# Rows of 1/rms for two RMS norms: by TensorE, or by a store and a repeated load through DRAM

## The chip, the cores and the metric

The kernel runs on one core of a Trainium2 chip. Its engines are TensorE (PE in the profile; its weight loads are PEld), VectorE (DVE), ScalarE (ACT), GpSimd (POOL, hardly used here) and SyncE (SP), which issues nearly all DMAs. The core has 16 DMA engines. The metric is device time in microseconds (us) of one execution, of which the median of several runs is taken. A profiled execution gives the trace; it has a time of its own, and a span, from its first to its last instruction.

## The reference

One layer of a streaming encoder, with 1024 positions and 1024 channels, in float32. What matters here:

```python
def rms_norm(x, w):
    x32 = x.astype(jnp.float32)
    y = x32 * lax.rsqrt(jnp.mean(x32 * x32, axis=-1, keepdims=True) + RMS_EPS)
    return (y * w.astype(jnp.float32)).astype(x.dtype)
...
h = rms_norm(x, norm1_w[l])
proj = h @ w_in[l]          # q, k, v, gates and branches: 8192 columns
...                         # retention heads, RG-LRU branch, merge
x = x + mix @ w_out[l]
h = rms_norm(x, norm2_w[l])
up = h @ ffn_w_up[l]
gate, val = jnp.split(up, [D_FF], axis=-1)
gate = causal_depthwise_conv(gate, ffn_conv_w[l], ffn_conv_b[l])
x = x + (jax.nn.gelu(gate) * val) @ ffn_w_down[l]
...
return rms_norm(x, norm_f_w)
```

There are three norms. The change touches how the first two get their factor 1/rms, one number for each of the 1024 positions, to where it is used.

## The kernel before, in words

**Layout.** Activations lie transposed: channels on the 128 partitions, positions along the free dimension, in two halves of 512. Each float32 operand of a large product is split into a rounded high part (on ACT, line 766) and a low part, the difference (on DVE, line 767), and every product is three passes: high by high, high by low, low by high. The large products go as jobs (`mm_fast`), each of 256 output channels by 1024 positions; a job makes 7 block products instead of 8 (a Strassen-like scheme) with sums of blocks of the weights (lines 811 to 818) and of the activations (`tsets`, `h2_steps`). A product is 12 matmuls (line 893) of 128 by 128 weights on 512 columns. A job uses three PSUM banks of six, and its results are taken out of PSUM by ACT and DVE (lines 900, 905, 914 and the job's own `emit`).

**Stages in order.** First x is loaded, both transposed (`xt`, for the operands) and plain (`x`, for the sums of squares, line 1121). The v columns of the input projection run first (`values_first`, line 1483), with the operand not yet scaled by 1/rms, since in v the positions are the output's partitions and the factor is applied behind the product. Four groups of 96 matmuls are made there, on two halves of positions and two halves of columns; in each, the weights come in eight slices of k. Meanwhile the factor is worked out and the transposed x is multiplied by the weight and by the row of 1/rms (`rescale`, line 1090), and its blocks, sums and splits are the operand h1 of the other input columns. Then come 24 jobs of the input projection, with the retention heads and the recurrent blocks spread between them, eight jobs of the two branch projections, and four of the output projection. In the last, x1 (the new residual stream) is turned back by PE transposes, stored, and its squares are summed by position (lines 1669 to 1675). The second norm is applied late: the 24 jobs of the up projection run on x1 with only the weight applied, and each result is multiplied by the row of 1/rms afterwards (`with_row`, line 1399, one multiplication for each 128 channels by 1024 positions). The convolution (lines 1737 to 1739), GeLU and the product with the other half follow, and 12 jobs of the down projection with the third norm end the kernel.

**How 1/rms becomes a row.** The factor r is made with positions on partitions: a [128, 8] tile, where r[p, t] belongs to position 128 t + p (`rstd_of`, lines 989 to 995). The row that is needed has all 1024 positions along the free dimension, the same on all 128 partitions (`rowt`). `rows_of` (line 1070) gets it with PE: for each of the eight t, DVE multiplies the identity by the column r[:, t] (line 1078), and PE multiplies a matrix of ones with this diagonal matrix, as a plain float32 matmul of 128 columns (line 1079); four of them fill one PSUM bank, and ACT copies each of the two banks into a half of `rowt` (line 1080). It is called once for the first norm (line 1125) and once for the second (line 1719).

**What sets the order.** No order is written by hand. Every operation is recorded with a cost and its dependencies, and a planner (`Prog`) simulates the engines, chooses the order of each engine's queue, gives out SBUF slots (105 of 512 columns) and PSUM banks, and emits that order; each engine then runs its queue strictly in order on the chip. An operation has a latest start, worked back from who needs it and from its slack; among operations that are ready, the one with the earliest latest start goes first. Main matmuls keep their recorded order, and "side" matmuls (such as those of `rows_of`) are put between them. A DMA is planned as landing no earlier than 2.3 us after issue (line 549), its data following the DMAs before it. `run` plans up to 12 times: after each pass `blame` moves operations ahead on which PE was seen to wait, the pass with the shortest planned span is kept, and after 6 passes without a better one it stops.

Of the kernel before, what the change touches and what calls it, by code (L numbers as in the profile page):

```python
# [17 lines left out]
ALU = mybir.AluOpType  # L18

P = 128  # L20
D = 1024
T = 1024
KT = 8
# [235 lines left out]
class Prog:  # L259
# [158 lines left out]
                    push(q)  # L418

    def run(self, caps):  # L420
        best, since = None, 0
        self.prune()
        for _ in range(self.ROUNDS):
            try:
                self.forward(caps)
            except RuntimeError as e:
                if best is None:
                    raise
                print(str(e)[:60])
                break  # L430
            since += 1
            if best is None or self.span < best[0]:
                best, since = (self.span, self.order, [(v, v.slot) for o in self.order for v in o.allocs], [
                    (o, o.start, o.allocs) for o in self.order]), 0
            if since >= self.PATIENCE:
                break
            self.blame()
        self.span, self.order, slots, starts = best
        for v, i in slots:
            v.slot = i  # L440
        for o, t, a in starts:
            o.start, o.allocs = t, a
        return self.order
# [195 lines left out]
    EAGER = 12000  # L639
    EARLY = 20000  # L640
    FETCH = 24000
    ROUNDS, PATIENCE, STALL, URGE = 12, 6, 150.0, 6000.0
    BEGIN = 400
    TILE = 800.0
    LAND = 1900.0
# [8 lines left out]
    def emit(self, engines, make, behind):  # L654
        at, sent = {}, []
        for o in self.order:
# [17 lines left out]
SMALL = (("par", (P, NPAR)), ("cst", (P, NCONST)), ("st", (P, 16)), ("nst", (P, 7, 8)), ("lt", (P, 2, 8)),  # L674
         ("state0", (P, 256)), ("state1", (P, 256)), ("bst", (P, 4, 6)),
         ("mv", (P, 4, 2)), ("rs", (P, 3, 4)), ("rowt", (P, T)))
SPILL = (("og", (KT, P, T)), ("u", (KT, P, T)), ("y", (KT, P, T)), ("sg", (2, KT, P, T)), ("t1", (KT, P, T)),
         ("x1", (T, D)), ("td", (3, 4, 2, P, 2, TH)), ("to", (2, 4, 2, P, 2, TH)), ("ff", (3, 8, P, 2, 4, P)), ("rot", (4, P, T)),
         ("ss", (12, 2, P, T)), ("v", (2, KT, P, TH)))

# [20 lines left out]
TSLACK = 8000.0  # L701
# [24 lines left out]
def record(prog, fx):  # L726
    V, S, G, PE, SY = (Engine(prog, n) for n in ("DVE", "ACT", "POOL", "PE", "SP"))
    par, cst, st, nst, lt = (fx[n] for n in ("par", "cst", "st", "nst", "lt"))
    rst, bst, mv, rs = fx["rst"], fx["bst"], fx["mv"], fx["rs"]
    og_d, u_d, y_d, sg_d, t1_d, x1_d, td_d, to_d, ff_d, rot_d, ss_d, v_d = (  # L730
        fx[n + "_d"] for n in ("og", "u", "y", "sg", "t1", "x1", "td", "to", "ff", "rot", "ss", "v"))
    x, positions, normf, w_in, w_v, w_ro, w_lo, w_out, w_up, w_dn, w_gate, out, xt = (
        fx[n] for n in ("x", "positions", "normf", "w_in", "w_v", "w_ro", "w_lo", "w_out", "w_up", "w_dn", "w_gate", "out", "xt"))
    ident = cst[:, C_ID:C_ID + P]
# [4 lines left out]
    def sm():  # L739
        return Ref(VT("sm", (P, P), F32, "sc"))  # L740

    def bank(kind="g"):
        return Ref(VT(kind, (P, TH), F32, kind))

    def pc(name, i):
        return par[:, PCOL[name] + i:PCOL[name] + i + 1]

    def cut(t, h):
        if h is None:
            return t  # L750
        return t[:, h] if len(t.shape) == 3 else t[:, TH * h:TH * h + TH]
# [4 lines left out]
    @contextmanager  # L756
    def within(slack, side=False):
        was = prog.slack, prog.side
        prog.slack, prog.side = slack, side
        yield  # L760
        prog.slack, prog.side = was
# [305 lines left out]

    row = {0: fx["rowt"]}

    def rows_of(r, side, slack=1000.0):  # L1070
        one = sm()
        V.memset(one, 1.0)
        for h in range(2):
            with within(slack, side):
                ps = bank()
                for t in range(4):
                    dg = sm()
                    V.tensor_scalar(dg, ident, r[:, 4 * h + t:4 * h + t + 1], None, ALU.mult)
                    PE.matmul(ps[:, 128 * t:128 * t + 128], one, dg, start=True, stop=True)  # L1079
                S.copy(cut(row[0], h), ps)  # L1080

    def scaled_split(t, w, name):
        hi, lo = get(name + "h", t.shape, F32R), get(name + "l", t.shape, F32R)
# [8 lines left out]
    def start_transposed():  # L1092
        if UNI:
            q = {(kh, h, jp): get("xq", PAIR) for h in range(2) for kh in range(2) for jp in range(2)}
            for h in range(2):
                for k in range(KT):
                    t = q[k // 4, h, k % 4 // 2][:, k % 2]
                    SY.dma_start(t, xt[h, k])
                    S.activation(t, t, AF.Copy, scale=pc("norm1_w", k))
                    b = f"B{k // 4 + 1}{h + 1}"  # L1100
                    if b != "B12" or STD_L:
                        h1[b, k % 4] = split(t, "h")
            for jp in range(2):
                b11, b12, b21, b22 = (q[kh, h, jp] for kh in range(2) for h in range(2))
                V.tensor_sub(b11, b11, b12)
                V.tensor_sub(b12, b22, b12)
                V.scalar_tensor_tensor(b22, b11, -1.0, b22, ALU.mult, ALU.subtract)
                V.scalar_tensor_tensor(b21, b22, -1.0, b21, ALU.mult, ALU.subtract)
                for n, t in (("T1", b11), ("T2", b22), ("T3", b12), ("T4", b21)):
                    put(h1, n, jp, split(t, "b", True))  # L1110
        q = [get("xq", QUAD) for _ in range(0 if UNI else 4)]
        for h in range(0 if UNI else 2):
            for k in range(KT):
                t = q[k // 2][:, k % 2, h]
                SY.dma_start(t, xt[h, k])
                h1u[f"B{k // 4 + 1}{h + 1}", k % 4] = scaled_split(t, pc("norm1_w", k), "h")
        prog.floor = FLOOR1
        for t in range(8):
            b = get("xs", FLAT)
            SY.dma_start(b, x[128 * t:128 * t + 128, :])  # L1120
            S.activation(b, b, AF.Square, accum_out=nst[:, 0, t:t + 1])
        a, r, w = (nst[:, i, 0:8] for i in range(3))
        V.tensor_scalar(a, a, 1.0 / D, EPS, ALU.mult, ALU.add)
        rstd_of(r, a, w)
        rows_of(r, True)
        if not UNI:
            for k in (0, 1, 4, 5, 2, 3, 6, 7):
                rescale(q, k, "norm1_w")
            operand(h1, of_quads(q), ("B11", "B21", "B22"), False)
            tsets(h1, of_quads(q))  # L1130
        prog.floor = -1e9
# [291 lines left out]
    og, u = {}, {}  # L1423
# [86 lines left out]
    for what in SEQ.split():  # L1510
        if what == "g":
            w, n = gates.pop(0)
            to = store(lambda m, w=w, n=n: sg_d[w, 2 * n + m])
# [5 lines left out]
        elif what[0] == "y":  # L1519
            n = int(what[1])  # L1520
            to = store(lambda m, n=n: y_d[2 * n + m])
# [4 lines left out]
        elif what[0] == "x":  # L1526
            n = int(what[1])
# [9 lines left out]
    one, ps = warm = sm(), bank()  # L1537
# [159 lines left out]
    for h in range(2):  # L1697
# [10 lines left out]
        with within(TSLACK, True):  # L1708
            a, b, c, e = (nst[:, i, 4 * h:4 * h + 4] for i in range(4))
            v, r = nst[:, 5, 4 * h:4 * h + 4], nst[:, 4, 4 * h:4 * h + 4]  # L1710
# [5 lines left out]
                V.tensor_add(v, v, e)  # L1716
            V.tensor_scalar(v, a if RELOAD else v, 1.0 / D, EPS, ALU.mult, ALU.add)
            rstd_of(r, v, a)
    rows_of(nst[:, 4, :], True, max(1000.0, TSLACK))
    if UNU:  # L1720
        pass
    elif UNS:
# [3 lines left out]
    else:  # L1726
        for h in range(2):
            for k in range(KT):
                t = x1q[k // 2][:, k % 2, h]
# [109 lines left out]
def tile_trunk_layer(ctx, tc, x, positions, params, consts, normf, w_in, w_v, w_ro, w_lo,  # L1839
# [9 lines left out]
    fx["rst"] = [fx.pop("state0"), fx.pop("state1")]  # L1849
    for n, shape in SPILL:  # L1850
        fx[n + "_d"] = Ref(Fixed(pdr.tile(list(shape), F32, tag=n, name=n + "_d"), shape))
# [83 lines left out]
```

## Time and profile before

| what | value |
|---|---|
| median of 3 runs | 1589.55 us (1587.86 to 1590.51) |
| the profiled execution: time | 1588.03 us |
| the profiled execution: span | 1586.2 us |
| PE busy | 1576.6 us, 99% |
| DVE busy | 1267.2 us, 80% |
| ACT busy | 869.7 us, 55% |
| moved by DMA | 294.51 MB, mean 186 GB/s |
| granted PE clock, mean | 0.999 |

Busy time is the time in which an engine has an instruction running; for PE, whose matmuls overlap, it says that there is always one in flight, not that it runs at its highest rate. A line of the timeline has the start, the length (of a merged run of the same instruction, whose count stands at the end), the engine, the line of the code, the operation, and the tiles with an arrow from inputs to output. A line of an engine's idle time ends with what it waited for, in square brackets. SPq is SP's queue of DMA issues; a DMA's time to landing is counted from its issue.

### The profile page before, as it was taken

The page shows a single profiled execution, that of the slowest core. Times are in us where ns is not written, and L with a number is a line of the kernel's source. Part 1 is how long each engine was busy: PE and PEld are TensorE (multiplying, and loading weights), DVE is VectorE, ACT ScalarE, POOL GpSimd, SP SyncE. Part 2 cuts the span into 40 slices and gives each one's busy share as a digit, 9 for nine tenths or more (in the row PEclk, how much of TensorE's full clock was granted, in tenths as well). Part 3 has the DMA queues.
Part 4 walks back from the last instruction along what each step waited for, and adds up shares of the span by engine and source line. Part 5 has one row for each costly group of instructions (what it writes and reads, how often), then busy time and mean ns, then how long its engine had stood idle before and what let it go on. Part 6 is the DMA issues. An engine that isn't in the chain of part 4 may idle for free.

```text
span 1586.2 us, 19156 instructions
## 1 busy us (share of the span) xinstructions
PE 1576.6 (99%) x7084; PEld 1307.0 (82%) x7084; DVE 1267.2 (80%) x1693; ACT 869.7 (55%) x1168; POOL 0.2 (0%) x4
## 2 busy tenths in 40 slices
PE   9999999999999999999999999999999999999998
PEld 8888888888888888888888888888888888888886
DVE  5995687887787888969795887788888787977795
ACT  7464468476457458645365954444444446454463
POOL 0000000000000000000000000000000000000000
PEclk9999999999999999999999999999999999999999
DMA  9325224436475757968344522456566425786761
GB/s 333 136 69 169 76 99 147 130 123 223 149 265 169 266 189 268 368 237 339 135 165 137 195 80 80 129 190 197 195 201 196 140 91 196 261 285 250 262 221 67
DMA packets 124253, 294.51 MB, mean 186 GB/s; under 512 B 9984, under 2 KB 38784, under 8 KB 124160
## 3 DMA queue, kind: packets, MB, share of 16 engines
q1 hardware_dynamic: 123728, 292.76, 53.5%
q8 instruction: 56, 0.92, 0.2%
q10 hardware_dynamic: 432, 0.53, 0.1%
q14 instruction: 37, 0.30, 0.1%
HBM read 202.02 MB, written 87.03 MB: 182 GB/s over the span
## 4 chain that ended last, share of the span: by engine, by line
PE 99%; ACT 0%; DMA 0%; DVE 0%; issue 0%; SPq 0%; ACTq 0%
PE g L893 87%; PE g L1483 6%; PE a L1270 3%; PE a L1353 1%; PE a L1360 1%; PE a L1352 1%; PE a L1346 0%; PE a L1663 0%; PE a L1389 0%; PE g L1079 0%; PE a L1324 0%; DMA xq<-xt 0%; PE g L1488 0%; ACT hh L1084 0%; ACT ub L1820 0%; ACT a L1801 0%
## 5 line engine op out<-in xcount | busy, mean ns | idle before, releaser
L893 PE MATMUL g<-bh,wh 128*128 128x512 f32 x1728 | 678.3, 393 | 0.7 <-ACT ua L900 0.7
L893 PEld LDWEIGHTS g<-bh,wh 128*128 128x128 f32 x1728 | 324.5, 188 | 67.4 <-ACT ua L900 1.1
L893 PE MATMUL g<-bh,wl 128*128 128x512 f32 x880 | 344.9, 392 | 0.0
L893 PE MATMUL g<-bl,wh 128*128 128x512 f32 x864 | 340.4, 394 | 0.0
L893 PE MATMUL g<-bh,wrr 128*128 128x512 f32 x824 | 322.0, 391 | 0.0
L766 ACT CAST wh<-wr 128x1024 fp32r<-128x1024 f32 (+1 forms) x220 | 198.7, 918 | 76.8 <-DVE wr L818 24.4
L893 PEld LDWEIGHTS g<-bh,wl 128*128 128x128 f32 x880 | 165.3, 188 | 33.5
L893 PEld LDWEIGHTS g<-bl,wh 128*128 128x128 f32 x864 | 162.4, 188 | 32.7
L767 DVE TENSOR_TENSOR wrr<-wr,wh 128x1024 fp32r<-128x1024 f32 (+1 forms) x154 | 152.1, 992 | 45.8 <-ACT wh L766 45.6
L893 PEld LDWEIGHTS g<-bh,wrr 128*128 128x128 f32 x824 | 154.7, 188 | 31.8
L766 ACT CAST wh<-ws 128x1024 fp32r<-128x1024 f32 x66 | 69.5, 1053 | 109.4 <-DVE ws L812 60.1
L893 PE MATMUL g<-tdr,wh 128*128 128x512 f32 x320 | 124.5, 389 | 0.0
L893 PE MATMUL g<-hl,wh 128*128 128x512 f32 x288 | 112.2, 389 | 0.0
L893 PE MATMUL g<-hh,wh 128*128 128x512 f32 x288 | 112.1, 389 | 0.0
L905 DVE TENSOR_TENSOR ub<-ub,g 128x512 f32<-128x512 f32 x72 | 49.4, 686 | 71.8 <-PE g L893 71.6
L767 DVE TENSOR_TENSOR wl<-wr,wh 128x1024 fp32r<-128x1024 f32 x66 | 80.6, 1221 | 14.1 <-ACT wh L766 11.5
L900 ACT ACTIVATE ub<-g 128x512 f32<-128x512 f32 x72 | 43.0, 597 | 81.6 <-PE g L893 74.4
L767 DVE TENSOR_TENSOR wl<-ws,wh 128x1024 fp32r<-128x1024 f32 x66 | 80.5, 1219 | 4.9 <-PE g L893 4.1
L893 PE MATMUL g<-tsr,wh 128*128 128x512 f32 x208 | 81.5, 392 | 0.0
L914 ACT ACTIVATE g<-g 128x512 f32<-128x512 f32 x72 | 42.0, 583 | 67.2 <-PE g L893 66.9
L905 DVE TENSOR_TENSOR ua<-ua,g 128x512 f32<-128x512 f32 x72 | 49.3, 685 | 29.2 <-PE g L893 27.7
L900 ACT ACTIVATE ua<-g 128x512 f32<-128x512 f32 x72 | 43.0, 597 | 50.8 <-PE g L893 47.3
(267 smaller groups left out, 2548.8 us busy)
## 6 DMA issues: line engine op xcount, KB each, us to landing
wr<-w_up SPq DMA_DIRECT2D x50, 512.0 KB, 4.0
wr<-w_in SPq DMA_DIRECT2D x48, 512.0 KB, 4.5
dw<-w_dn SPq DMA_DIRECT2D x42, 512.0 KB, 4.6
ff_d<-gc SPq DMA_DIRECT2D x24, 512.0 KB, 3.9
wr<-ff_d SPq DMA_DIRECT2D x24, 512.0 KB, 6.3
td<-td_d SPq DMA_DIRECT2D x24, 512.0 KB, 5.8
x<-x_d SPq DMA_DIRECT2D x24, 512.0 KB, 5.8
td_d<-dw SPq DMA_DIRECT2D x18, 512.0 KB, 5.9
```

The costliest lines, as they stand in the source:

```text
L766: S.copy(hi, src)
L767: V.tensor_sub(lo, src, hi.bitcast(F32))
L893: PE.matmul(ps, (hi, lo)[a][:, c], o[b], start=first and n == 0, stop=n == 11, skip_group_check=True)
L900: S.activation(cut(d[m], h), ps, AF.Copy, scale=scale)
L905: (V.tensor_sub if m else V.tensor_add)(u, u, ps)
L914: S.activation(Y, X, AF.Copy)
L1270: PE.matmul(ps, wg[a][:, g, cs], xs[b][:, k], start=q == 0, stop=q == 5)
L1352: PE.matmul(p2[:, 0:256], q[:, bs], rst[cur], start=True, stop=False)
L1353: PE.matmul(p2[:, 0:256], s, v, start=first, stop=True)
L1360: PE.matmul(p3[:, 0:256], kd[h][:, bs], v, start=True, stop=True)
L1483: PE.matmul(ps[t], a[i][:, 128 * t:128 * t + 128], b[j], start=k == 0 and i + j == 0, stop=k == KT - 1 and i == 1)
```

## The change

`rows_of` no longer uses PE. SP stores r from SBUF into a row in DRAM, so that position 128 t + p stands at its own place in the row; as r holds the positions of one t down the partitions, the store goes value by value. Then SP loads that row for all 128 partitions, straight into `rowt`. Both norms have a row of DRAM of their own. The load waits for the store, and both have no slack of their own in the plan. The planner's `run` is edited too: up to 6 passes instead of 12, no early stop, and a random bias on some operations, whose size (`JITTER`) is 0.

```diff
     def run(self, caps):
-        best, since = None, 0
+        best = None
         self.prune()
+        rng = np.random.default_rng(self.SEED)
+        for o in self.ops:
+            if o.eng != "PE" and all(v.kind == "u" for v in o.uses):
+                o.bias = self.JITTER * rng.random()
         for _ in range(self.ROUNDS):
             try:
                 self.forward(caps)
             except RuntimeError as e:
-                if best is None:
-                    raise
                 print(str(e)[:60])
                 break
-            since += 1
             if best is None or self.span < best[0]:
...
-            if since >= self.PATIENCE:
-                break
             self.blame()
...
-    ROUNDS, PATIENCE, STALL, URGE = 12, 6, 150.0, 6000.0
+    SEED, JITTER, ROUNDS, STALL, URGE = 0, 0.0, 6, 150.0, 6000.0
...
-SPILL = (("og", (KT, P, T)), ...
+SPILL = (("row", (2, 1, T)), ("og", (KT, P, T)), ...
...
-    def rows_of(r, side, slack=1000.0):
-        one = sm()
-        V.memset(one, 1.0)
-        for h in range(2):
-            with within(slack, side):
-                ps = bank()
-                for t in range(4):
-                    dg = sm()
-                    V.tensor_scalar(dg, ident, r[:, 4 * h + t:4 * h + t + 1], None, ALU.mult)
-                    PE.matmul(ps[:, 128 * t:128 * t + 128], one, dg, start=True, stop=True)
-                S.copy(cut(row[0], h), ps)
+    def rows_of(r, side, at):
+        with within(None, side):
+            SY.dma_start(row_d[at].rearrange("o (t p) -> p (o t)", p=P), r)
+            SY.dma_start(row[0], row_d[at].to_broadcast((P, T)))
...
-        rows_of(r, True)
+        rows_of(r, True, 0)
...
-    rows_of(nst[:, 4, :], True, max(1000.0, TSLACK))
+    rows_of(nst[:, 4, :], True, 1)
```

More of the change, by code (lines that the diff above doesn't have):

```diff
@@ L426, in run @@
             except RuntimeError as e:
-                if best is None:
-                    raise
                 print(str(e)[:60])
                 break
-            since += 1
             if best is None or self.span < best[0]:
-                best, since = (self.span, self.order, [(v, v.slot) for o in self.order for v in o.allocs], [
-                    (o, o.start, o.allocs) for o in self.order]), 0
-            if since >= self.PATIENCE:
-                break
+                best = (self.span, self.order, [(v, v.slot) for o in self.order for v in o.allocs], [
+                    (o, o.start, o.allocs) for o in self.order])
             self.blame()
@@ L676 @@
          ("mv", (P, 4, 2)), ("rs", (P, 3, 4)), ("rowt", (P, T)))
-SPILL = (("og", (KT, P, T)), ("u", (KT, P, T)), ("y", (KT, P, T)), ("sg", (2, KT, P, T)), ("t1", (KT, P, T)),
+SPILL = (("row", (2, 1, T)), ("og", (KT, P, T)), ("u", (KT, P, T)), ("y", (KT, P, T)), ("sg", (2, KT, P, T)), ("t1", (KT, P, T)),
          ("x1", (T, D)), ("td", (3, 4, 2, P, 2, TH)), ("to", (2, 4, 2, P, 2, TH)), ("ff", (3, 8, P, 2, 4, P)), ("rot", (4, P, T)),
@@ L729, in record @@
     rst, bst, mv, rs = fx["rst"], fx["bst"], fx["mv"], fx["rs"]
-    og_d, u_d, y_d, sg_d, t1_d, x1_d, td_d, to_d, ff_d, rot_d, ss_d, v_d = (
-        fx[n + "_d"] for n in ("og", "u", "y", "sg", "t1", "x1", "td", "to", "ff", "rot", "ss", "v"))
+    row_d, og_d, u_d, y_d, sg_d, t1_d, x1_d, td_d, to_d, ff_d, rot_d, ss_d, v_d = (
+        fx[n + "_d"] for n in ("row", "og", "u", "y", "sg", "t1", "x1", "td", "to", "ff", "rot", "ss", "v"))
     x, positions, normf, w_in, w_v, w_ro, w_lo, w_out, w_up, w_dn, w_gate, out, xt = (
```

## The prediction

> **What bounds the kernel now.** I read the page first, for the span and the chain that ended last, and then the table of busy time by stage, for the places where TensorE (PE) has idle time.
>
> ```profile
> span 1586.2 us, 19156 instructions
> ...
> PE 99%; ACT 0%; DMA 0%; DVE 0%; issue 0%; SPq 0%; ACTq 0%
> ```
>
> ```profile
> 5.00:42.00 37.00, 36.86 (x175) 30.58 (x176) 21.28 (x44) 28.82 (x49) 0.00 (x0) 1.00 0.99 348
> ...
> 400.00:700.00 300.00, 299.41 (x1362) 248.28 (x1361) 249.59 (x357) 180.33 (x240) 0.00 (x0) 1.00 0.68 240
> 700.00:900.00 200.00, 199.31 (x911) 164.75 (x910) 158.21 (x176) 114.37 (x151) 0.00 (x0) 1.00 0.56 197
> 900.00:930.00 30.00, 30.00 (x142) 25.12 (x141) 26.87 (x50) 19.84 (x38) 0.00 (x0) 1.00 0.27 95
> 930.00:1300.00 370.00, 370.00 (x1634) 306.39 (x1633) 301.74 (x322) 174.29 (x219) 0.00 (x0) 1.00 0.48 154
> ```
>
> The columns of the second view are the stretch, its length, then busy time and instructions of PE, PE's weight loads, DVE, ACT and POOL, then the granted clock, the DMA share and GB/s. PE is the chain for 99% of the span. In the five stretches shown it idles 0.14, 0.59, 0.69, 0 and 0 us. A matmul that overlaps the next can hide a gap inside its busy time, so the rate is the better test: from 930 to 1300 us there are 1634 matmuls in 370 us, one every 0.2264 us, with no gap. So the time is the number and size of the matmuls that PE is given, plus the start and the tail. A change pays if it takes work out of PE's queue, and costs if it makes PE wait. Nothing else counts directly.
>
> **What the change removes: PE work.** The view of line 1079 gives the matmuls that go, and PE's own timeline shows what they cost in its queue.
>
> ```profile
> L1079 PE MATMUL g<-sc,sc x32: 272/275/335, 36.4 to 922.3; 128*128 128x128 f32 x32
> ```
>
> ```profile
> 36.15 0.39 PE L1483 MATMUL g<-wh,hh 128*128 128x512 f32 x1
> 36.38 0.67 PE L1079 MATMUL g<-sc,sc 128*128 128x128 f32 x4
> ...
> 40.79 0.39 PE L1483 MATMUL g<-wh,hh 128*128 128x512 f32 x1
> ```
>
> ```profile
> 917.87 0.40 PE L893 MATMUL g<-hl,wh 128*128 128x512 f32 x1
> ...
> 922.67 0.39 PE L893 MATMUL g<-bh,wfr 128*128 128x512 f32 x1
> ```
>
> There are 32 records for 16 calls: each plain float32 matmul leaves two. Their durations (about 0.275 us) overlap, so 32 times 0.275 would be too much. I take start to start instead. From the L1483 matmul at 36.15 us to the one at 40.79 us PE starts 12 of the other, ordinary matmuls (the first counted, the last not); at 0.2264 us these need 2.72 us, and the stretch takes 4.64 us, so the row matmuls of the first norm cost 1.92 us. From 917.87 to 922.67 us there are 13 ordinary ones, 2.94 us of 4.80 us: the second norm costs 1.86 us. Together that is 3.78 us of PE's queue, which I round to 3.8 us. Nothing covers it: PE is the chain at both places, so all of it comes off the span, if PE finds its next operands ready.
>
> Also removed are the sixteen multiplications of the identity on DVE, four copies from PSUM on ACT, a memset and the use of one PSUM bank per half. They ran beside PE, and the copies' and multiplications' engines are not what it waits for; I count them at nothing.
>
> **What it adds: two DMAs in series for each norm.** SyncE (SP) issues a store of r and then a load of all 128 partitions from that one DRAM row. The load waits for the store's landing, and since SP takes its queue in order, everything behind the load waits too. In the store, neighbouring values of a partition land 128 values apart in DRAM, so it is 1024 separate values of 4 bytes, 64 for each of 16 DMA engines. No row of the trace has this form. The nearest rows:
>
> ```profile
> q1 hardware_dynamic: 123728, 292.76, 53.5%
> ...
> wr<-w_up SPq DMA_DIRECT2D x50, 512.0 KB, 4.0
> ...
> nf<-normf SPq DMA_DIRECT2D x1, 512.0 KB, 9.8
> ...
> par<-params ACTq DMA_DIRECT2D x1, 4.0 KB, 3.0
> ```
>
> Store, lower end: 3.0 us, the landing of the one other transfer of 4 KB (par). Upper end: SP's 123728 packets took 53.5% of 16 engines for 1586.2 us, 13578 us in all, 0.110 us each at a mean size of 2.4 KB; 64 in turn are 7.0 us, on top of the 3.0 us: 10.0 us. Load, lower end: 4.0 us as an ordinary 512 KB load (w_up); upper end: 9.8 us, as nf, which has the same form, one row of 4 KB read for 128 partitions. The chain of both is then 7.0 to 19.8 us. I take 5 us for the store, nearer to par, since 4 bytes should not hold an engine as long as 2.4 KB, and nf's 9.8 us for the load: about 15 us.
>
> On the price of single values I weigh one page against that row. The Trainium skill, "DMA: Bandwidth & Descriptors", section "Rules for kernel authors", says that a strided last dimension becomes one descriptor per element and should be rearranged to be contiguous. That speaks against this store; no run here shows it yet. With it the store would be at the upper end and not at the lower, and the sum would stay the same, as follows from the leads below.
>
> **Where this wait lies.** First norm:
>
> ```profile
> 35.20 0.16 DVE L995 TENSOR_TENSOR nst<-nst 128x8 f32<-128x8 f32 x1
> ...
> 44.54 3.67 DVE L1090 SCALAR_TENSOR_TENSOR xq<-xq,par,rowt 128x1024 f32<-128x1024 f32 x3
> 48.13 1.22 DVE L767 TENSOR_TENSOR wrr<-wr,wh 128x1024 fp32r<-128x1024 f32 x1
> ...
> 103.66 1.23 DVE L767 TENSOR_TENSOR tsr<-ts,bh 128x1024 fp32r<-128x1024 f32 x1
> ```
>
> ```profile
> 52.57 0.39 PE L1483 MATMUL g<-wrr,hh 128*128 128x512 f32 x1
> ...
> 123.29 0.39 PE L893 MATMUL g<-tsr,wh 128*128 128x512 f32 x1
> ```
>
> ```profile
> 37.70 0.42 SPq L1469 DMA_DIRECT2D wr<-w_v  x1
> ```
>
> r is ready at 35.36 us, so the row lands between 42.4 and 55.2 us. DVE first uses it at 44.54 us, and its queue is in order: it would stand for 0 to 10.7 us (about 6 with my values), with the weight splits and all h1 operands queued behind. The last operand made, tsr, ends at 104.89 us and PE first reads it at 123.29 us: a lead of 18.4 us. So even the longest wait is covered with 7.7 us left. On SP, the fourth load of w_v at 37.70 us can move behind the store by up to 10 us. Its split ran at 48.13 us. PE starts its group of 96 matmuls at about 52.57 us, and this weight is the last quarter, 72 matmuls or 16.3 us later, at 68.9 us. The split ends at 49.35 us, 19.5 us ahead; 10 us later is still early enough. In this stage the DMA engines are 0.99 busy, which speaks for the upper half of the chain's range.
>
> Second norm:
>
> ```profile
> 913.16 0.15 DVE L995 TENSOR_TENSOR nst<-nst 128x4 f32<-128x4 f32 x1
> ...
> 923.25 1.23 DVE L1399 TENSOR_TENSOR ua<-ua,rowt 128x1024 f32<-128x1024 f32 x1 [1.47 <-ACT rowt L1080]
> ...
> 936.42 1.22 DVE L767 TENSOR_TENSOR wl<-ws,wh 128x1024 fp32r<-128x1024 f32 x1
> ```
>
> ```profile
> 953.95 0.39 PE L893 MATMUL g<-bh,wl 128*128 128x512 f32 x1
> ```
>
> r is ready at 913.31 us and the row lands between 920.3 and 933.1 us; its first use was at 923.25 us. DVE stands for 0 to 9.9 us (about 5), and with it ACT, whose convolution step takes DVE's result, and behind both the evacuations and the weight splits. The split wl, by the names and the order of the jobs, ends at 937.64 us and is read at 953.95 us: 16.3 us of lead, 6.4 us more than the longest wait. The w_up loads behind the store on SP come later by as much as SP stands; this uses up the same lead, it doesn't add to it. What is late next after the row matmuls is the next ordinary matmul: PE's queue simply closes up.
>
> **The edit of the planner.** JITTER is 0, so the random bias adds nothing. The number of planning passes falls from at most 12 to 6 with the best kept. Since operations vanish, the whole order is planned anew in any case, and the SBUF slots with it. I cannot price this from a row except from one side: PE idles 0.59 and 0.69 us between 400 and 900 us, so a better order has 1.3 us to win there, and a worse one has no limit. I take 0.
>
> **Sum.** The profiled execution took 1588.03 us, 1.83 us more than its span. Less 3.8 us it is 1584.2 us. The median of the three runs shown is 1589.55 us, 1.5 us above the profiled one; less 3.8 us it is 1585.8 us, my forecast. Its own range is 1584.4 to 1587.2 us, plus and minus half the spread of the three runs (1587.86 to 1590.51). About 0.2% (3.2 us here, so below 1586.4 us) is what a measurement of this kernel can tell from no change; the gain is 0.24%, only just beyond it.
>
> **Rivals.** First, *the gain is partly given back*: a new order, or a late row in an order with shorter leads, leaves PE idle for 1 to 6 us more. For it speaks that the planner is told 2.3 us at least for a store (line 549), less than the 3.0 us of par, so it queues DVE work that needs the row too early; against it the leads above. With 2.5 us of idle the time is 1588.3 us: no change.
>
> Second, and slower: *the row comes later than the leads allow*. The place is DVE's wait ahead of L1090 and L1399. It decides from a chain of 27.6 us in the first norm (35.36 plus 27.6, less 44.54, is 18.4) and of 26.2 us in the second. From there each us costs one us of PE, in each norm. At a chain of 30.4 us the two lose 2.8 and 4.2 us, in all 3.2 us more than the gain: 1592.8 us. The single values in a busy queue speak for it, both nearest rows against it: it needs half as much again as the upper end. By the page's rule on strided elements its chance rises only if a packet of 4 bytes takes longer than one of 2.4 KB.
>
> Third, and slower too: *the six passes end on an order with holes*. With over 7.0 us of idle beyond before's 1.3 us in the middle of the span the time passes 1592.8 us; at 10 us it is 1595.8 us. For it: fewer passes, an order no one has seen. Against it: DVE and ACT lie well below PE in every stretch from 400 us on, so an order without holes is not rare.
>
> **How the numbers follow.** Forecast 0.62, of which 0.12 falls within 0.2% by the scatter of medians, as the gain exceeds the bound by just 0.6 us. Partly given back: 0.21, all within. The late row: 0.05; holes: 0.10; both slower. A better order that also takes the 1.3 us: 0.02, faster. So faster is 0.52, same 0.33, slower 0.15. The low end, 1583.2 us, is the better order (1585.8 less 1.3) with the scatter of 1.3 us; the high end, 1592.0 us, takes in the whole of the first rival and leaves out most of the two slow ones: about 0.15 above and 0.03 below.
>
> **What would show it.** Right: no L1079 on PE; ordinary matmuls every 0.2264 us through the places where the rows were made; between the store's issue and the landing of the load 7 to 20 us; DVE idle ahead of L1090 and L1399 put down to the DMA of rowt, while PE stays busy through both stages; the span 3.8 us shorter. Wrong: gaps on PE at 95 to 125 or 930 to 955 us (the late row), or idle time on PE anywhere else that before didn't have (the new order), or a chain beyond 26 us.

## The result and the profile after

The changed kernel takes 1599.32 us (median of 4 runs, 1596.96 to 1600.48), beside it the kernel before 1589.99 us (median of 4 runs): a ratio of 1.006, with a 95% interval of 1.0044 to 1.0075. It is slower by 9.3 us, where a gain of 3.8 us was forecast, and lies above the range.

The profiled execution took 1600.12 us, and its span is 12.1 us longer than the one before. The head of the page and its chain of waits:

```profile
span 1598.3 us, 19038 instructions
...
PE 94%; DMA 3%; DVE 1%; ACT 1%; issue 0%; SPq 0%; ACTq 0%; DVEq 0%
```

PE was 99% of the chain before. Now DMA has 3% of it, DVE and ACT 1% each. The view of PE's waits (instruction, what it waited for, us in total, times, longest) shows where:

```profile
PE g L892 <- ACT g L913: 8.7, 1, 8.7
PE g L1475 <- ACT v L1487: 3.5, 1, 3.5
```

Two waits are new and large, and both are for ACT, on lines that take a result out of a PSUM bank. (Line numbers after the edit are smaller by 1 or by 8: L892 is L893 of before, L913 is L914, L1391 is L1399, L1475 is L1483, L1487 is L1495.) PE's timeline at the second norm:

```profile
937.39 0.39 PE L892 MATMUL g<-bh,wl 128*128 128x512 f32 x1
946.51 0.79 PE L892 MATMUL g<-bh,wh 128*128 128x512 f32 x1 [8.73 <-ACT g L913]
947.10 0.63 PE L892 MATMUL g<-bl,wh 128*128 128x512 f32 x1
947.53 0.63 PE L892 MATMUL g<-bh,wl 128*128 128x512 f32 x1
...
951.68 0.39 PE L892 MATMUL g<-hh,wh 128*128 128x512 f32 x1
```

and at the first:

```profile
51.59 0.39 PE L1475 MATMUL g<-wh,hl 128*128 128x512 f32 x1
55.51 0.50 PE L1475 MATMUL g<-wh,hh 128*128 128x512 f32 x1 [3.53 <-ACT v L1487]
55.84 0.39 PE L1475 MATMUL g<-wrr,hh 128*128 128x512 f32 x1
```

Start to start tells the cost. At the second norm 9.12 us pass where 0.23 us are needed: 8.9 us lost. Then the 12 matmuls from 946.51 to 951.68 us take 5.17 us; at 0.2264 us each they would take 2.72 us: another 2.45 us, at about half rate. At the first norm 3.92 us pass instead of 0.23 us: 3.7 us lost, with a rate that is back at once. The table of stretches (length, busy time and instructions of PE, PEld, DVE, ACT and POOL, granted clock, DMA share, GB/s) has the same for the second norm: 61.27 us of 70 busy, at a mean clock of 0.93. The second line is the stretch in which the trace has the clock granted at one half: 10.24 us, which begin 3.5 us into the gap and end as the matmuls are back at full rate.

```profile
930.00:1000.00 70.00, 61.27 (x261) 50.18 (x260) 50.94 (x56) 32.01 (x40) 0.00 (x0) 0.93 0.31 97
...
941.29:951.53 10.24, 5.02 (x12) 3.96 (x13) 9.66 (x11) 5.95 (x8) 0.00 (x0) 0.50 0.48 154
```

So the account is: 3.8 us saved on PE, as forecast; 3.7 us lost at the first norm; 11.3 us at the second. That is 11.2 us more, of 12.1 us by the spans; the rest, under 1 us, is the balance of small waits that came and went.

What made ACT late is seen in SP's timeline (start, length of the issue) and in the view of DMA issues (KB each, median us to landing):

```profile
35.10 0.38 SPq L1071 DMA_DIRECT2D row_d<-nst  x1
...
38.67 0.90 SPq L1461 DMA_DIRECT2D wr<-w_v  x1
50.65 0.32 SPq L1072 DMA_DIRECT2D rowt<-row_d  x1
...
916.16 0.36 SPq L1071 DMA_DIRECT2D row_d<-nst  x1
928.75 0.33 SPq L1072 DMA_DIRECT2D rowt<-row_d  x1
```

```profile
wr<-w_v SPq DMA_DIRECT2D x4, 512.0 KB, 10.8
...
rowt<-row_d SPq DMA_DIRECT2D x2, 512.0 KB, 4.7
row_d<-nst SPq DMA_DIRECT2D x2, 4.0 KB, 14.1
```

The load is issued as soon as the store has landed, so the store of 4 KB took 15.5 us in the first norm and 12.6 us in the second. The repeated load took a median of only 4.7 us. And the four loads of w_v, a median of 6.2 us in the kernel before, now take 10.8 us. The chain of waits in order of time (start, us, what), first norm:

```profile
38.67 15.16 DMA wr<-w_v
...
53.92 0.04 ACT wh L765
...
54.88 0.59 ACT v L1487
...
55.51 4.61 PE g L1475 x19
```

Here PE doesn't wait for the row. A load of w_v, issued while the store is under way, takes 15.2 us; ACT's split of that weight (L765) waits for it; behind that split in ACT's queue stand the copies of v (L1487), whose PSUM bank PE needs next. The table of stretches shows the DMA engines 0.88 busy there at only 42 GB/s; in the kernel before it is 0.22 at 85 GB/s in the same stretch.

```profile
42.00:48.00 6.00, 6.00 (x29) 4.95 (x28) 1.11 (x2) 0.00 (x0) 0.00 (x0) 1.00 0.88 42
```

Second norm:

```profile
916.16 12.57 DMA row_d<-nst
...
933.87 1.24 DVE ua L1391
...
935.13 1.26 ACT gc L1729
...
944.73 1.24 ACT gc L1729
945.97 0.49 ACT g L913
...
946.51 13.51 PE g L892 x48
```

The row comes 17.6 us after r. DVE's multiplication (L1391) waits for it, ACT's convolution step (L1729) for DVE, twice over, since two products have piled up. Behind the second step, in ACT's queue, stands L913, the evacuation of an unrelated product, which needs nothing of the row. PE waits for its bank.

### The profile page after: what moved, and what is told of

Read it like the earlier page. It is cut to its first block, busy times and chain, and to the rows that moved or that the text cites. A ratio compares the mean times of both kernels' runs of the same rounds, so it can differ in the third digit from the quotient of the medians.

```text
span 1598.3 us, 19038 instructions
## 1 busy us (share of the span) xinstructions
PE 1576.5 (99%) x7052; PEld 1305.8 (82%) x7052; DVE 1261.3 (79%) x1675; ACT 862.2 (54%) x1164; POOL 0.2 (0%) x4
## 2 busy tenths in 40 slices
DMA packets 126620, 295.55 MB, mean 185 GB/s; under 512 B 12096, under 2 KB 40896, under 8 KB 126528
## 4 chain that ended last, share of the span: by engine, by line
PE 94%; DMA 3%; DVE 1%; ACT 1%; issue 0%; SPq 0%; ACTq 0%; DVEq 0%
PE g L892 83%; PE g L1475 5%; PE a L1262 3%; DMA wr<-w_v 1%; PE a L1345 1%; DMA row_d<-nst 1%; PE a L1352 1%; PE a L1344 1%; DMA vt<-v_d 1%; PE a L1338 0%; PE a L1381 0%; PE a L1655 0%; DMA rowt<-row_d 0%; PE a L1316 0%; DMA par<-params 0%
## 5 line engine op out<-in xcount | busy, mean ns | idle before, releaser
L892 PE MATMUL g<-bh,wh 128*128 128x512 f32 x1728 | 679.7, 393 | 8.7 <-ACT g L913 8.7
L892 PEld LDWEIGHTS g<-bh,wh 128*128 128x128 f32 x1728 | 325.1, 188 | 75.8 <-ACT g L913 9.1
L892 PE MATMUL g<-bh,wl 128*128 128x512 f32 x880 | 345.6, 393 | 0.0
L892 PE MATMUL g<-bl,wh 128*128 128x512 f32 x864 | 340.7, 394 | 0.0
L892 PE MATMUL g<-bh,wrr 128*128 128x512 f32 x824 | 321.9, 391 | 0.0
L765 ACT CAST wh<-wr 128x1024 fp32r<-128x1024 f32 (+1 forms) x220 | 198.5, 916 | 78.7 <-DMA wr<-w_up 23.4
L892 PEld LDWEIGHTS g<-bh,wl 128*128 128x128 f32 x880 | 165.9, 188 | 33.9
L892 PEld LDWEIGHTS g<-bl,wh 128*128 128x128 f32 x864 | 163.0, 189 | 32.4
L892 PEld LDWEIGHTS g<-bh,wrr 128*128 128x128 f32 x824 | 154.7, 188 | 31.9
L892 PE MATMUL g<-tdr,wh 128*128 128x512 f32 x320 | 124.5, 389 | 0.0
L765 ACT CAST wh<-ws 128x1024 fp32r<-128x1024 f32 x66 | 69.3, 1050 | 94.7 <-DVE ws L811 43.9
L892 PE MATMUL g<-hl,wh 128*128 128x512 f32 x288 | 112.2, 390 | 0.0
L892 PE MATMUL g<-hh,wh 128*128 128x512 f32 x288 | 112.0, 389 | 0.0
L892 PE MATMUL g<-tsr,wh 128*128 128x512 f32 x208 | 81.7, 393 | 0.0
L913 ACT ACTIVATE g<-g 128x512 f32<-128x512 f32 x72 | 42.0, 583 | 71.8 <-PE g L892 71.6
```

Source lines behind the costliest of these rows:

```text
L765: S.copy(hi, src)
L892: PE.matmul(ps, (hi, lo)[a][:, c], o[b], start=first and n == 0, stop=n == 11, skip_group_check=True)
L913: S.activation(Y, X, AF.Copy)
```

## The experiments

The theory after the result has two parts. The store of single values is slow by its own form, and because ACT works in order, its lateness reaches PE by way of PSUM banks, with a far shorter lead than the one that was counted. The rivals: that the new plan's order is worse in itself, or the planner's edit; that a two-step path through DRAM is too slow in any form; that the store is slow because it stands in SP's queue; and, on the store's price, that it goes by the number of values. Each expectation below says in its own words which theory it speaks of. All ratios are to the kernel before on the same chip.

**The planner's edit alone.** The whole new `run` and its settings, with `rows_of` left as before.

```diff
-        best, since = None, 0
+        best = None
...
-    ROUNDS, PATIENCE, STALL, URGE = 12, 6, 150.0, 6000.0
+    SEED, JITTER, ROUNDS, STALL, URGE = 0, 0.0, 6, 150.0, 6000.0
```

> The kernel before with only the planner's edit (at most 6 passes, no early stop, a bias of size 0); the rows are made by TensorE. Theory: the order comes out as it was, so the time is that of before, ratio 1.000. Rival B (the planner's edit cost part of the loss): 1592 us or more.

1589.0 us beside 1589.26 us, ratio 1.0002 (0.9993 to 1.0011). The order of the instructions came out the same as before, instruction for instruction. This part of the change is worth nothing.

**The same DMAs with the store in 128 runs of 8 values.** r goes to DRAM as it lies, position 128 t + p at place 8 p + t, and DVE reads the loaded row in steps of 8.

```diff
+    def by_t(d):
+        return d.rearrange("q (p t) -> q t p", t=8)
...
-            SY.dma_start(row_d[at].rearrange("o (t p) -> p (o t)", p=P), r)
+            SY.dma_start(row_d[at].rearrange("o (p t) -> p (o t)", p=P), r)
...
-        V.scalar_tensor_tensor(t, t, pc(name, ch), row[0].rearrange("p (h c) -> p h c", h=2), ALU.mult, ALU.mult)
+        t = t.rearrange("p h (t c) -> p (h t) c", t=4)
+        V.scalar_tensor_tensor(t, t, pc(name, ch), by_t(row[0]), ALU.mult, ALU.mult)
...
-            V.tensor_mul(t, t, row[0])
+            w = t.rearrange("p (t c) -> p t c", t=8)
+            V.tensor_mul(w, w, by_t(row[0]))
```

> The order of all instructions is that of the changed kernel; only the store's form and the way DVE reads the row differ: 128 runs of 8 values in place of 1024 single values. Theory A (the single values are slow to store, 12.6 to 15.5 us, and PE starves behind that at both norms, 3.85 us and 11.3 us by PE's own timeline): the store lands in 2.3 to 4 us, PE has no gap at either norm, and the time is 1599.3 less 15.2, about 1584 us, 6 us below before. Rival B (the new order of the plan has the holes): the time stays at about 1599 us. Rival C (the wait of SP and the repeated load of one row are what is slow, whatever the store): less than half comes back, 1592 us or more.

1590.12 us beside 1589.06 us, ratio 1.0007 (0.9998 to 1.0016). The order of every engine is that of the changed kernel. The store now lands in 5.8 and 1.4 us, and both gaps of PE are gone, so the order has no holes of its own and the path through DRAM isn't too slow as such. But the gain isn't there either. One row of the groups by form says why:

```profile
L1396 DVE TENSOR_TENSOR ua<-ua,rowt 128x1024 f32<-128x1024 f32 x24 | 51.3, 2139 | 0.3
```

With its second operand read in steps of 32 bytes the multiplication takes 2.14 us; in the changed kernel it took 1.22 us. DVE has 50 us more to do (1311.5 us of busy time, 1261.3 us in the changed kernel), and PE waits in many small places.

**One norm at a time.** The first keeps the single values in norm 1, the second in norm 2; the other norm has runs of 8 and the read in steps.

```diff
+            SY.dma_start(row_d[at].rearrange("o (t p) -> p (o t)", p=P) if at == 0 else    # the second kernel: at == 1
+                         row_d[at].rearrange("o (p t) -> p (o t)", p=P), r)
```

> As the run with runs of 8 values, but in the second norm alone; the first norm keeps the 1024 single values. Theory A: the gap of 11.3 us of the second norm goes, that of the first (3.85 us) stays: 1588.0 us. Rival B: 1599 us. Rival C: 1594 us or more.

1589.07 us beside 1589.06 us, ratio 1.0005 (0.9996 to 1.0014).

> As the run with runs of 8 values, but in the first norm alone; the second keeps the 1024 single values. Theory A: the gap of 3.85 us of the first norm goes, that of the second stays: 1595.5 us. If the two gaps share a cause further on in the kernel, the two single-norm runs do not add up to the run of both. Rival B: 1599 us.

1595.92 us, ratio 1.0046 (1.0033 to 1.006). So the second norm's store carries most of the loss. These two also give the lead on ACT by measurement. The chain of the second norm, with the single values:

```profile
913.24 11.00 DMA row_d<-nst
...
924.26 4.71 DMA rowt<-row_d
```

From the store's issue to the row it is 15.7 us here and PE waits 6.8 us; in the changed kernel, in the same order, it is 17.6 us and PE waits 8.7 us. By these two points each microsecond more costs one, and the wait begins at a chain of 8.9 us in both. In the first norm the w_v load landed at 51.95 us with the first of these kernels and PE waited 1.5 us; in the changed kernel it landed at 53.83 us and PE waited 3.5 us: one for one again.

**The fast store and the plain read together.** As the kernel with runs of 8, but the row is read as it lies, so the factors go to wrong positions; the work, and the order of every engine, is the changed kernel's in every other respect.

> The order of all instructions is that of the changed kernel. The store is 128 runs of 8 values, so that the row in DRAM is in another order, and DVE reads it as it lies, without the strided access of the run with runs of 8 values: the factors go to the wrong positions, only the time counts. Theory A' (the single values made the loss, and the strided read, 2.13 us in place of 1.22 us for each of 48 multiplications and 2.2 in place of 1.28 for eight, ate what the store gave back): PE's 3.8 us appear at last, about 1585 us. Rival B' (the new order of the plan has small holes of its own worth some 5 us, which the faster store lays bare): 1590 us, as with the strided read.

1584.4 us beside 1589.03 us, ratio 0.997 (0.9959 to 0.9982). The span is 1580.9 us, and in PE's waits only 1.4 us are left, 1.0 us of them at the start. SP's timeline at the second norm:

```profile
910.13 0.33 SPq L1071 DMA_DIRECT2D row_d<-nst  x1
911.54 0.33 SPq L1072 DMA_DIRECT2D rowt<-row_d  x1
```

The store lands in 1.4 us in place of 12.6 us. With nothing else changed the forecast gain is there (4.6 us by the medians; beyond the 3.8 us, this kernel also has fewer small waits than the one before, 1.4 us against 2.6 us in the views of PE's waits). Taken with the last three kernels this settles it: the loss is the form of the store, and 3.8 us was a fair price for PE's work.

**The store by itself, in several forms.** A kernel of DMAs alone, no layer. Each form twice, with a dependent load behind each.

```python
for k, nm in ((8, "all"), (4, "half"), (2, "quarter"), (1, "eighth")):
    SP.dma_start(q.rearrange("o (t p) -> p (o t)", p=P), r)     # 128 k single values, side by side in DRAM
...
SP.dma_start(q[:, 0:1].rearrange("(t p) o -> p (t o)", p=P), r)   # "apart": 1024 single values, 64 bytes apart
...
SP.dma_start(q.rearrange("o (p t) -> p (o t)", p=P), r)           # "runs": 128 runs of 8
```

> Leaves out the whole layer: copies x to the output and stores and loads rows one after the other with nothing else in flight, each twice: 1024, 512, 256 and 128 single values side by side, 1024 single values 64 bytes apart, 128 runs of 8, then 1024 single values with an independent load of 512 KB issued right behind on SP's queue, or at the same time on ACT's queue, and that load alone. Theory A (a price per single value): about 12.5 us from issue to landing for 1024, and about 2.5 us plus 10 us times the share for the others, so 7.5, 5 and 3.8 us; 128 runs of 8 as 128 single values; 64 bytes apart as side by side. If neighbouring values in the same 64 bytes wait for each other, 64 bytes apart is much faster. A load behind on SP's queue lands some 10 us later than alone if the store holds the DMA engines or the queue; on ACT's queue it is late only if the engines themselves are held.

The DMA issues, us to landing, first of the two rounds:

```profile
allone<-srca SPq DMA_DIRECT2D x1, 4.0 KB, 8.7
...
eighthone<-srcd SPq DMA_DIRECT2D x1, 0.5 KB, 7.2
apartone<-srce SPq DMA_DIRECT2D x1, 4.0 KB, 2.7
...
runsone<-srcf SPq DMA_DIRECT2D x1, 4.0 KB, 1.4
```

The theory of a price for each value falls. An eighth of the values costs almost as much (7.2 us, 7.0 us the second time), while all 1024 set 64 bytes apart take 2.7 us. It isn't how many values are written, but what lies next to them. A load of 512 KB issued 0.4 us behind the store on SP's queue landed after 12.1 and 12.6 us, in place of 3.3 us by itself. (A load put on ACT's queue beside the store told nothing, as it was issued 0.2 us ahead of it.)

**How near is too near.** Again DMAs alone: single values 8, 16, 32 and 64 bytes apart, runs of 2, 4 and 8 side by side, each followed by a load that waits for it, so that the time from issue to issue is the store's.

> Leaves out the whole layer, like the first run of stores alone; each twice, nothing else in flight: 1024 single values 8, 16, 32 and 64 bytes apart, runs of 2, 4 and 8 values side by side, four stores of 8 runs of 32 values, and a load of 512 KB behind 1024 single values 64 bytes apart on SP's queue. There, 64 bytes apart took 2.7 us and side by side 8.4 to 12 us. If writes into the same 32 bytes wait for each other: 32 bytes apart is as fast as 64 (2.7 us), 16 and 8 apart are slow by 2 and 4 writes per 32 bytes (about 3.5 and 5 us), runs of 2 and 4 values as these. If the unit is 64 bytes: 32 apart is slower too. The load behind the values 64 bytes apart lands in 4 to 6 us, not in 12 us, if it is the same wait that held it there; in about 12 us if it is the count of 1024 values.

SP's timeline has each store and the load that waits for it, here for 8 bytes apart: 20.02 less 15.62 is 4.40 us.

```profile
15.62 0.38 SPq L41 DMA_DIRECT2D gapbone<-srca  x1
20.02 0.37 SPq L42 DMA_DIRECT2D back<-gapbone  x1
```

| form | writes into the same 32 bytes | issue to issue, us, both turns |
|---|---|---|
| values side by side (4 bytes apart; from the kernel above) | 8 | 8.8, 8.4 |
| 8 bytes apart | 4 | 4.40, 4.54 |
| 16 bytes apart | 2 | 3.02, 3.30 |
| 32 bytes apart | 1 | 2.61, 2.68 |
| 64 bytes apart | 1 | 2.62, 2.63 |
| runs of 2 (8 bytes) | 4 | 4.10, 4.18 |
| runs of 4 (16 bytes) | 2 | 3.01, 2.23 |
| runs of 8 (32 bytes) | 1 | 1.47, 1.50 |

The time goes by the number of writes that fall into the same 32 bytes of DRAM, from 32 bytes on the distance no longer matters, and the number of writes matters little beside it. A load behind the values 64 bytes apart on SP's queue landed in 4.6 us, and the four stores of 8 runs of 32 values, which a kernel further down uses, took 2.2 and 2.4 us together. The reading is that writes into one 32-byte unit are served one after the other; these times can't show by which part of the memory path.

**Does the slow store hold other transfers?** An independent transfer of 512 KB, 2.7 to 2.9 us behind the store, from SP's queue or from ACT's. "Gap" is the store with values 64 bytes apart.

> Leaves out the whole layer, like the other runs of stores alone; each twice. A store of 1024 single values side by side on SP's queue, and some 2.5 us after it an independent transfer of 512 KB: a load on SP's queue, a load on ACT's queue, a store on SP's queue, a store on ACT's queue, and that last one again with the single values 64 bytes apart, where they are quick. Theory Q (what is behind on the same queue is held): load and store on SP land after some 10 us or more, both on ACT after 3 to 5 us. Theory E (the DMA engines are held for everyone): all four land after some 10 us, and only the one behind the values 64 bytes apart in 3 to 5 us. Theory W (the write side of the engines is held): the stores land late on both queues, and the load on ACT's queue, which writes to SBUF, may do so too.

```profile
big<-w SPq DMA_DIRECT2D x2, 512.0 KB, 10.2
big<-w ACTq DMA_DIRECT2D x2, 512.0 KB, 9.9
...
storeactonefar<-pause ACTq DMA_DIRECT2D x1, 512.0 KB, 9.0
...
storeactgaponefar<-pause ACTq DMA_DIRECT2D x1, 512.0 KB, 2.6
```

A load takes 10.2 us behind it on SP and 9.9 us on ACT; a store takes 9.1 us on SP and 9.0 us on ACT, and 2.6 us behind the spread values. The queue doesn't matter: whatever follows, load or store, lands 0.9 to 3.5 us after the slow store is through and not before, as theory E has it. The w_v load of the first norm did the same, with 3.2 us (the store landed at 50.6 us, the load at 53.8 us).

**The store issued by ACT.**

```diff
-            SY.dma_start(row_d[at].rearrange("o (t p) -> p (o t)", p=P), r)
+            S.dma_start(row_d[at].rearrange("o (t p) -> p (o t)", p=P), r)
```

> The changed kernel with the store of 1024 single values issued from ACT's queue, the repeated load still from SP's. Theory (in the first norm the slow store holds SP's own DMA queue, so that the load of w_v behind it lands 15.2 us after issue): the four w_v loads land in 7 us or less as before, PE's gap of the first norm goes; the second norm's row is as late as it was, with a gap of 8 to 11 us, so about 1595 us. If the store holds the DMA engines for everyone, w_v is as late as before and the time stays at 1599 us.

1596.87 us, ratio 1.0052 (1.0036 to 1.0069). It didn't tell apart what it was meant to: the plan's order differs, and the last w_v load was issued only at 49.00 us, after a wait of 10.2 us for the row's store, since the program gives its DMA semaphores out in turn and this load had the same one as the store. The store was as slow as from SP (10.9 us in the second norm), so it isn't SP's queue that makes it slow.

**The plan told the truth.** The changed kernel with the store entered in the planner as landing after 15.5 us and holding the DMA for 13.5 us.

```diff
-            o.lat = 2700 + max(0, size - 262144) / 262144 * 800
+            o.lat = 15500 if size == 4096 else 2700 + max(0, size - 262144) / 262144 * 800
...
+                if o.dma == 4096 and o.eng == "SP":
+                    lat = max(lat, 15500.0)
+                    dma_free = max(dma_free, t + 13500.0)
```

> The changed kernel with the store of 1024 single values, but the planner's price for that store is 15.5 us to landing, and 13.5 us in which no other DMA goes on, in place of 2.3 us; so it puts other work ahead of what needs the row. If the loss is that engines stand in order behind a row planned too early, the time comes near to before or below, 1585 to 1590 us, with the store as slow as it is. If the slow store starves PE whatever the order, it stays at 1595 us or more.

1589.27 us, ratio 1.0003 (0.9993 to 1.0012). The store is as slow as ever (12.2 and 11.7 us in SP's timeline), but work that needs nothing of the row now stands ahead of the work that waits for it, and PE's longest wait is 1.9 us. That wait is followed by 3.41 us at half the granted clock; both together are some 3.6 us by estimate, which is nearly the gain of 3.8 us. In the second norm the evacuation that stood behind the row in the changed kernel (L913, here L916) now waits for PE's own product:

```profile
935.87 0.58 ACT L916 ACTIVATE g<-g 128x512 f32<-128x512 f32 x1 [0.23 <-PE g L895]
```

So nearly the whole loss can be planned around, though not with the gain kept.

**A version that beats both kernels.** DVE turns r within blocks of 32 by 32, so that a partition holds 32 neighbouring positions, and four stores write 8 runs of 128 bytes each. The row in DRAM is in its plain order (laid out as [8, 4, 32] for each norm), and DVE reads it plainly; `rt` and `tr` are tiles of 128 by 32.

```diff
-            SY.dma_start(row_d[at].rearrange("o (t p) -> p (o t)", p=P), r)
-            SY.dma_start(row[0], row_d[at].to_broadcast((P, T)))
+            V.tensor_copy(rt[:, 0:8], r)
+            V.transpose(tr, rt)
+            for b in range(4):
+                SY.dma_start(row_d[at, :, b], tr[32 * b:32 * b + 8, :])
+            SY.dma_start(row[0], row_d[at].rearrange("(o t) b i -> o (t b i)", o=1).to_broadcast((P, T)))
```

> The computation is whole. DVE transposes r in blocks of 32 by 32 first, so that each DMA row is 32 values long and in the right order: four stores of 8 runs of 128 bytes, then the repeated load, and DVE reads the row as it lies. Theory A': no PE gap at either norm, 3.8 us below before, about 1585.3 us, give or take 1.5 us for a plan made anew. Rival B' (plans made anew lose a few us of themselves): 1588 us or more. Rival C (SP's wait and the repeated load are slow in any form): 1592 us or more.

1585.34 us (1584.47 to 1586.21) beside 1589.03 us, ratio 0.9978 (0.9969 to 0.9986): faster than the kernel before by 3.7 us. SP's timeline and PE's waits:

```profile
914.85 1.30 SPq L1076 DMA_DIRECT2D row_d<-tr  x4
...
917.27 0.33 SPq L1077 DMA_DIRECT2D rowt<-row_d  x1
```

```profile
PE g L1538 <- DVE st L1540: 1.0, 1, 1.0
...
PE g L892 <- ACT g L913: 0.3, 1, 0.3
```

The four stores are through 2.4 us after the first issue (5.1 us in the first norm). The wait for L913, 8.7 us in the changed kernel, is 0.3 us here.

## Why the prediction was wrong, point by point

**What bounds the kernel, and PE's saving: right.** No L1079 is left on PE, and the two kernels with a fast store and a plain read gain about what start to start gave: spans of 1583.6 and 1580.9 us against 1586.2 us, medians 3.7 and 4.6 us below the kernel before. The planner's edit was rightly taken at 0, and the load was overestimated (9.8 us taken, 4.7 us measured).

**The store's price: wrong.** The step was "I take 5 us for the store, nearer to par", with 10.0 us as the upper end. It measured 15.5 and 12.6 us. The upper end priced 64 packets in turn on an engine by the mean packet of the kernel, and the choice of 5 us rested on 4 bytes not holding an engine as long as 2.4 KB. The trace's packet records agree with that, but it isn't what counts: in the second norm all packets of the store begin between 917.0 and 917.8 us and take a median of 0.007 us, yet the store lands at 928.7 us. What counted was something that none of the nearest rows had: eight writes into the same 32 bytes. The rule quoted there from the Trainium skill, "DMA: Bandwidth & Descriptors", section "Rules for kernel authors", was borne out. The packets under 512 bytes number 12096 in the changed kernel and 10304 with runs of 8; the difference, 1792, is 896 for each norm, as many as 1024 elements are more than 128 runs. The rule gives no time, and so the warning was weighed as if it were only a count.

**What the store holds: missed.** The prediction moved the fourth w_v load later on SP "by up to 10 us" and asked only when its split is read. The load was issued nearly in time, at 38.67 us in place of 37.70 us, and then took 15.2 us: in the kernel of DMAs alone, too, what follows the slow store lands only after it.

**The leads: wrong, and this alone would have turned the gain into a loss.** The step was "16.3 us of lead, 6.4 us more than the longest wait", read from DVE's split wl to the matmul that uses it. That lead may be as long as it says; it isn't the shortest. The prediction even named what stands behind DVE, "and behind both the evacuations and the weight splits", and then followed only the splits. In the second norm the chain of 17.6 us lies inside its bounds of 7.0 to 19.8 us (by luck, as a store priced too low and a load priced too high offset each other), and yet PE stood still; with its own middle value, about 15 us, the measured threshold of 8.9 us gives a wait of 6.1 us, more than the gain of 3.8 us. The kernel before shows the short lead. On ACT:

```profile
934.65 0.58 ACT L914 ACTIVATE g<-g 128x512 f32<-128x512 f32 x1
```

and on PE, the first matmul of the product that takes over the bank (by its place in the order, the one that stood still after the change):

```profile
937.17 0.39 PE L893 MATMUL g<-bh,wh 128*128 128x512 f32 x1
```

The evacuation ends at 935.23 us, 1.9 us ahead of PE. From 923.25 us, where DVE first used the row, to that evacuation ACT and DVE alternate almost without a pause. The row could then come 9.9 us after r (923.25 less 913.31) as before, some 1.9 us later by this lead, and 1.9 us sooner since PE arrives that much earlier: about 9.9 us, by estimate, against 8.9 us measured.

**The rival of the late row: the right direction and the wrong threshold.** That it decides from a chain of 27.6 us in the first norm and of 26.2 us in the second came from the same leads. In the second norm it decides from 8.9 us; in the first, PE was stopped by the held load, not by the row. The rival of an order with holes is refuted: the same order, with a fast store and a plain read, leaves PE no gap to speak of.

**After the gap.** No step allowed for matmuls at half rate; it cost 2.45 us.

What stays open: in the second norm the table of stretches shows no DMA packet at work (share 0.00) from 918 us to 928 us, though the store lands only at 928.7 us, so what the store waits for there isn't visible. And the part of ACT's order was shown by the chain, by the one-for-one threshold and by its vanishing with a fast store; an order of ACT with only the evacuation moved ahead wasn't tried, though the kernel with the truthful plan comes near to it.

## What to carry to other kernels

Before counting a store in bytes or in descriptors, look at which writes share 32 bytes of DRAM: if neighbouring positions lie on different partitions, turn them on the chip first, so that each partition writes a run. When an operand comes later, find the shortest lead, not the obvious one: go along every in-order engine that the wait stops, and ask of each queued instruction, evacuations of PSUM above all, when PE needs what it frees. A slow transfer must be priced with what runs beside it on the DMA engines, whichever queue that came from.

## What the runs showed of the hardware

Writes of a DMA into the same 32 bytes of DRAM slow each other down: 1024 single values take 8.4 to 12.0 us side by side with little else running, 12.6 and 15.5 us in the changed kernel, and 2.6 us from 32 bytes apart on; 128 runs of 32 bytes take 1.4 us. While such a store runs, a transfer of 512 KB from another queue takes 9 to 10 us, in place of 3.3 us for a load by itself and 2.6 us for a store behind the spread values.

After a gap PE may run at half the clock, and the gap's length alone doesn't decide it. In the kernel with the store on ACT, a gap of 2.0 us in the first norm was followed by this:

```profile
54.42 0.50 PE L1475 MATMUL g<-wh,hh 128*128 128x512 f32 x1 [2.04 <-ACT v L1487]
...
57.62 0.63 PE L1475 MATMUL g<-wh,hl 128*128 128x512 f32 x1
58.04 0.52 PE L1475 MATMUL g<-wh,hh 128*128 128x512 f32 x1
```

```profile
54.90:58.31 3.41, 3.41 (x10) 2.63 (x9) 3.41 (x7) 0.93 (x2) 0.00 (x0) 0.50 0.30 112
```

with starts 0.43 us apart, while after the 3.5 us gap of the changed kernel the rate was back with the second matmul. The gaps of 5.6, 6.8 and 8.7 us all had such a stretch, of 8 to 13 matmuls, and so had the 1.9 us gap of the kernel with the truthful plan. In the traces' clock records these stretches last 3.41, 6.83 or 10.24 us, and every change of the clock falls on a grid of 3.41 us steps that runs through the whole execution. Laid on this grid, the five stretches each follow a step in which PE idled for 1.91 us or more (1.91, 2.04, 2.27, 2.39 and 3.41 us), and no step with up to 1.84 us of idle time at the full clock was followed by one. The 3.5 us gap fell across the edge of two steps, 1.84 us in one and 1.69 us in the other. That a step's idle time decides is a reading of these few gaps, not an experiment.

The Trainium skill, "TensorE: Matmul & The Clock Gate", Part 1, gives 426.7 ns from start to start for 512 columns on the idle clock, and a window of about 3.4 us that runs freely; the 0.427 us and the grid agree. The same page, section "Why this matters for your kernels", advises to avoid gaps over about 3 us; that isn't a bound on the safe side here, as 1.9 us was enough.

A DVE multiplication of 128x1024 float32 values whose second operand is read in steps of 32 bytes takes 2.14 us in place of 1.22 us.
